# Mixture sums in PSUM, earlier weights for the last merge row, and a re-timed residual scaling in a hybrid encoder layer

## The chip, the core and the metric

One core of a Trainium2 chip runs the whole layer in one launch. The metric is the device time of a run in microseconds (us), lower is better. PE is TensorE, DVE VectorE, ACT ScalarE, POOL GpSimd, SP the engine that issues the DMAs.

## What is computed

1,024 positions of 1,024 channels pass through one layer: two parallel branches (latent attention A, and RWKV-7 time mixing B), a gated mixture, a merge, and a gated MLP with a three-tap convolution. All of it is fp32. The part that matters here:

```
gates = sigmoid(gate_cols + b_gate)
x = x + (gates[0] * y_a + gates[1] * y_b) @ w_merge
h = rms_norm(x, norm_ffn_g)
gp = dwconv_centered(h @ w_ffn_gate, ffn_conv_w, ffn_conv_b)
x = x + (silu(gp) * (h @ w_ffn_up)) @ w_ffn_down
```

with y_a = A @ w_o[:512] and y_b = B @ w_o[512:].

## The kernel before

Activations lie with channels on the 128 partitions, positions along the free dimension. A **row** below is one tile of 128 output channels by 1,024 positions; it fills two PSUM banks of 512 positions. fp32 precision comes from splitting: each operand x becomes hi = x rounded to fp32r (a copy on ACT) and lo = x - hi (a subtraction, `split`, line 211), and each product is three matmuls, hi*hi, hi*lo, lo*hi. A weight tile is loaded raw (`wraw`), ACT makes `whi`, POOL makes `wlo` (`wload`, line 217); raw, hi and lo have two buffers each.

After both branches, gates[0]*y_a lies in DRAM as eight rows `d_y0`, and the gate logits as `d_gate`. The stages that the change touches:

- **Mixture**, `mixture(j)`, line 1641, rows j = 0 to 7. It loads y0 and the gate logits gt (two buffers each, used in turn), and multiplies four k-tiles of B by w_o (`product`, line 1377). In `branch` (line 1394) ACT takes the sigmoid of gt in place, and DVE multiplies the two PSUM banks into gt. Then DVE adds y0, ACT copies the sum to `yh`, and DVE subtracts for `yl`. Until `yl` is done, gt is not free for the load of row j+2.
- **Merge**, the loop at line 1711: row j is eight k-tiles of yh, yl times w_merge, 48 matmuls of 512 columns, in two weight halves of four k-tiles. `residual` (line 1707) adds x (loaded into `x2` at line 1658); ACT and DVE then make scaled and split forms for the FFN (`scaled`, `sums`) and squares for the norm (`squares`). Row 7 is written apart (line 1772), behind row 6's followers.
- **FFN**, 22 hidden tiles f. Each gate and up tile is computed by a scheme of seven quarter products on sums and differences of weight and activation blocks (U1 to U4, B11 to B22), made by DVE and POOL. `ones` times `acc` sums the squares; ACT forms irs = sqrt(mean + eps) and rs2 = 1/irs by Ln and Exp. `over` (1826) multiplies the rows of x2 by irs on POOL, since the result is multiplied by rs2 at the very end; `into` (1869) adds the down product of a row to x2, so row j must be scaled ahead of it (rows 0 to 3 in f = 2, rows 4 to 7 in f = 3). `taps` (two DVE operations over 1,023 columns), `silu`, `left` and `right` form the hidden tile.

PSUM has two sets of four banks, and `big4` (1636) takes a pair from one set and the other in turn. The second set opens at line 1653, behind row 1, so row 3 gets row 0's banks, and a later row j those of row j-4.

The order of PE is the order of the code. Up to the end of merge row 6 a scheduler orders the other engines by readiness and free buffers; from line 1733 on all engines follow the code. Each engine, and SP's queue of DMA issues, runs in order.

Of the kernel before, what the change touches and what calls it, by code (L numbers as in the profile page):

```python
# [13 lines left out]
AF = mybir.ActivationFunctionType  # L14
# [5 lines left out]
D = 1024  # L20
# [66 lines left out]
def block_kernel(ctx: ExitStack, tc: tile.TileContext, a):  # L87
# [64 lines left out]
    def act(out, in_, func, **kw):  # L152
        name = SETS.get(func)
        if name is None:
            return S.activation(out, in_, func, **kw)
        if name != cur["set"]:
            ld = S.preload_act_table_set(name)
            if "ordered" in cur:
                cur.update(set=name)
                return S.activation(out, in_, func, **kw)  # L160
            for g in cur["group"]:
                tc.add_manual_dep(ld.ins, g.ins.name, NOSYNC, reason="table set order")
            if cur["load"] is not None and not cur["group"]:
                tc.add_manual_dep(ld.ins, cur["load"].ins.name, NOSYNC, reason="table set order")
            cur.update(set=name, load=ld, group=[])
        i = S.activation(out, in_, func, **kw)
        if "ordered" in cur:
            return i
        tc.add_manual_dep(i.ins, cur["load"].ins.name, NOSYNC, reason="table set order")
        cur["group"].append(i)  # L170
        return i
# [39 lines left out]
    def split(x, hi, lo, eng=None):  # L211
        S.copy(hi, x)
        (eng or G).tensor_tensor(out=lo, in0=x, in1=hi.bitcast(F32), op=sub)
# [508 lines left out]
    def parts(idle=False):  # L722

        while True:
            e = None
            for i, (live, run, todo, pace) in enumerate(lanes):
                while len(run) < live and todo:
                    run.append([now[0], todo.pop(0), i])
                for x in run:
                    if e is None and (idle or now[0] >= last[i] + pace) and (x[0] in rkv if isinstance(x[0], tuple) else x[0] <= now[0]):  # L730
                        e = x
            if e is None:
                if not idle or not any(run for _, run, _, _ in lanes):
                    return
                now[0] = min(e[0] for _, run, _, _ in lanes for e in run)
                continue
            i = e[2]
            last[i] = now[0]
            x = next(e[1], None)
            if x is None:  # L740
                lanes[i][1].remove(e)
            else:
                e[0] = x if isinstance(x, tuple) else now[0] + DELAY[x]
# [625 lines left out]
    first = []  # L1369

    def wrows(src, k, n):
        return wload(src[:, k * 128:min(k + 4, n) * 128], 128 * min(4, n - k), bufs=2)
# [21 lines left out]
    def branch(br, j, xs, ps, gt):  # L1394

        if br:
            gate_load(br, j, gt)
        for k, ns in enumerate(product(ps, w_o(br, j), xs, NPAIR, br == 0)):
            if k == (1 + br):
                act(gt, gt, AF.Sigmoid, bias=vc("bgate", 8 * br + j))  # L1400
            elif k == 3:
                for x, hs in zip(ps, HT):
                    V.tensor_tensor(out=gt[:, hs], in0=x, in1=gt[:, hs], op=mult)
            yield ns

    fetched = []
# [229 lines left out]
    def big4():  # L1636
        nps[0] += 1
        return [psc[nps[0] % len(psc)].tile([128, 512], F32, tag="b4", name="b4") for _ in HT]

    sP.close()  # L1640
    def mixture(j):

        y0 = bq.tile([128, T], F32, tag=f"b{j % 2}", name="y0")
        nc.sync.dma_start(y0, d_y0[j])
        y = bq.tile([128, T], F32, tag=f"b{2 + j % 2}", name="gt")
        yield from branch(1, j, xs, big4(), y)
        V.tensor_tensor(out=y, in0=y, in1=y0, op=add)
        split(y, *yx[j], V)

    two_ = [mixture(j) for j in range(2)]  # L1650
    for i in (0, 0, 0, 1, 1, 1, 0, 0, 1, 1):
# [55 lines left out]
    def residual(j, ps):  # L1707
        for p, hs in zip(ps, HT):
            V.tensor_tensor(out=p, in0=p, in1=x2[j][:, hs], op=add)

    for j in range(7):
        ps = big4()
        for _ in product(ps, a["w_merge"][j], yx):
            pass
        residual(j, ps)
        k, g = j % 4, vc("gffn", j)
        y1, y2_ = ps
        scaled((B11 if j < 4 else B21)[k], y1, g)
        if j < 4:
            d = t5("p1")  # L1720
            S.copy(d, y1)
            V.tensor_tensor(out=d, in0=y2_, in1=d, op=sub)
            scaled(U1[k], d, g)
        else:
            t3, t2 = sums(j, ps, scaled_b12(j))
            split(t3, *U3[k], V)
            split(t2, *U2[k], V)
            scaled(B22[k], y2_, g)
        squares(j, ps)
# [95 lines left out]

    def over(js):
        for j in js:
            G.tensor_tensor(out=x2[j][:, :], in0=x2[j][:, :], in1=irs, op=mult)

    def load_next(f):  # L1830
        x11 = load("w_fu", f, 0, f5("AA"))
# [91 lines left out]
    e0()  # L1923
    e1 = u4(1)
    w7a = parts(s3)
    e1()
    bb1 = db[0]
    quarter(bb, w6a, U2, True)
# [2 lines left out]
    e2 = u4(2)  # L1931
    w7b = parts(b21)
    e2()
    for hs, b in zip(HT, db[1:]):
        act(irs[:, hs], b, AF.Ln, scale=1.0 / D, bias=eps)
    G.tensor_tensor(out=s2, in0=a12, in1=s2, op=sub)
    G.tensor_tensor(out=s1b, in0=b12, in1=s1b, op=sub)
    quarter(bb1, w6b, U2, True)
    spare = fp.tile([128, T], F32, tag="sh", name="u2b", bufs=3)
    u2b, u3b = (spare[:, hs] for hs in HT)  # L1940
# [3 lines left out]
    quarter(bb, w7a, U3)  # L1944
    e3()
    w4a = parts(a22)
    act(rs2, irs, AF.Exp, scale=-0.5)
    act(irs, irs, AF.Exp, scale=0.5)
    quarter(bb1, w7b, U3)
    u3a = t5("u3")  # L1950
    V.tensor_tensor(out=u3a, in0=bb, in1=p1a, op=add)
# [33 lines left out]
    right(0, ba[0], bc[0], u2a, lambda: W.append(parts(x[1])))  # L1985
    u2 = t5("u2")
    V.tensor_tensor(out=u2, in0=bb, in1=p1, op=add)
    over((0, 1))
    taps(1, u, 0)
    taps(1, u, 1)  # L1990
    s22 = x[2]
# [2 lines left out]
    for f in range(2, NF):  # L1994
        b, c, last = ba[f % 2], bc[f % 2], f == NF - 1
        f0, j0 = (f // 2 - 1) * 2, f % 2 * 4
        d2 = load_down(f0, j0 + 2)
        if f > 2:
            quarter(b, W.pop(0), B11, True)
            right(f - 1, ba[1 - f % 2], bc[1 - f % 2], u2, lambda: W.append(parts(s3)))  # L2000
            quarter(bb, W.pop(0), U2, True)
            p1 = t5("p1")
            S.copy(p1, b)
            W.append(parts(d1, G))
            u2 = t5("u2")
            V.tensor_tensor(out=u2, in0=bb, in1=p1, op=add)
        else:
            W.append(parts(d1, G))
            silu(1)
            left(1, ba[1])  # L2010
            right(1, ba[1], bc[1], u2b)
        quarter(b, W.pop(0), B21)
        G.tensor_tensor(out=s2, in0=x12, in1=s2, op=sub)
        W.append(parts(s1))
        if f < 4:
            over(((2, 3), (6, 7))[f - 2])
        if last:
            d1 = load_down(NF - 2, 0)
        quarter(bb, W.pop(0), U3)
        W.append(parts(s22))  # L2020
        u3 = t5("u3")
        V.tensor_tensor(out=u3, in0=bb, in1=p1, op=add)
        W.append(parts(d2, G))
        if last:
            d2 = load_down(NF - 2, 2)
        else:
            x = load_next(f + 1)
        for v in units(W.pop(0), j0):
            e = dbank()
            for k in range(2):  # L2030
                down(v, f0, k, e)
            into(v, e)
        quarter(c, W.pop(0), U1, True)
        W.append(parts(s2))
        if not last:
            s1 = sums_next(*x)
        V.tensor_tensor(out=u3, in0=c, in1=u3, op=add)
        u = u22(u3)
        quarter(bb, W.pop(0), U4)
        W.append(parts(d1, G) if last else parts(x[0]))  # L2040
        if last:
            d1 = load_down(NF - 2, 4)
        else:
            s2 = diffs_next(x[0], x[1], s1)
        if f == 2:
            over((4, 5))
        u21(u, bb, p1)
        if not last:
            W.append(parts(s2))
        center(f, u)  # L2050
        todo = []
        for v in units(W.pop(0), j0 + 2):
            e = dbank()
            for k in range(2):
                down(v, f0, k, e)
            todo.append((v, e))
            if len(todo) < 3:
                into(*todo[-1])
                taps(f, u, len(todo) - 1)
            else:  # L2060
                into(*todo[-1])
        if last:
            W.append(parts(d2, G))
            d2 = load_down(NF - 2, 6)
        else:
            x12 = load("w_fu", f + 1, 1, f5("AA"))
            d1 = load_down(((f + 1) // 2 - 1) * 2, (f + 1) % 2 * 4)
        quarter(c, W.pop(0), B22)
        W.append(parts(d1, G) if last else parts(x12))
        silu(f)  # L2070
        left(f, b)
        s3, s22 = x[1], x[2]
# [115 lines left out]
```

## Time and profile before

| what | us |
|---|---|
| median of 3 runs (lowest, highest) | 1938.6 (1937.78, 1941.22) |
| the profiled execution, its own time | 1937.92 |
| its span, first to last instruction | 1936.1 |
| PE busy (share of the span) | 1841.8 (95%) |
| DVE, ACT, POOL busy | 1229.6, 871.1, 655.4 |
| mean granted TensorE clock | 0.974 of full |

The profile lists for each engine its instructions in order of time, with the idle time ahead of one and the engine whose work ended it. A lost microsecond counts only where PE, or what PE waits for, is on the chain that ended last. The mixture runs from about 1103 to 1149 us of the span, the merge from there to 1251, the first FFN steps to 1334.

### The profile page before, as it was taken

The page shows a single profiled execution, that of the slowest core. Times are in us where ns is not written, and L with a number is a line of the kernel's source. Part 1 is how long each engine was busy: PE and PEld are TensorE (multiplying, and loading weights), DVE is VectorE, ACT ScalarE, POOL GpSimd, SP SyncE. Part 2 cuts the span into 40 slices and gives each one's busy share as a digit, 9 for nine tenths or more (in the row PEclk, how much of TensorE's full clock was granted, in tenths as well). Part 3 has the DMA queues.
Part 4 walks back from the last instruction along what each step waited for, and adds up shares of the span by engine and source line. Part 5 has one row for each costly group of instructions (what it writes and reads, how often), then busy time and mean ns, then how long its engine had stood idle before and what let it go on. Part 6 is the DMA issues. An engine that isn't in the chain of part 4 may idle for free. (4 is left out here: it accounts for less than half of the span.)

```text
span 1936.1 us, 36734 instructions
## 1 busy us (share of the span) xinstructions
PE 1841.8 (95%) x14928; PEld 1467.8 (76%) x14928; DVE 1229.6 (64%) x1837; ACT 871.1 (45%) x1380; POOL 655.4 (34%) x558
## 2 busy tenths in 40 slices
PE   6889999999999999989999999988999999999998
PEld 5657666888788877767777777767888888888886
DVE  7567665445556686766573264687766757667567
ACT  5676567223233565655666444442323333233231
POOL 7435554421222333352533322236222222222321
PEclk9989999999999999997999999999999999999999
DMA  4135544954555645453435672101111111111112
GB/s 158 37 120 193 181 157 147 252 140 99 142 144 122 148 110 137 101 139 84 104 83 174 213 250 87 55 33 55 50 56 59 49 50 52 63 50 50 49 55 103
DMA packets 260632, 210.65 MB, mean 109 GB/s; under 512 B 127144, under 2 KB 205032, under 8 KB 260464
## 3 DMA queue, kind: packets, MB, share of 16 engines
q1 hardware_dynamic: 260464, 208.31, 36.4%
q8 instruction: 117, 1.92, 0.4%
q14 instruction: 51, 0.42, 0.1%
HBM read 144.64 MB, written 59.41 MB: 105 GB/s over the span
## 5 line engine op out<-in xcount | busy, mean ns | idle before, releaser
L108 POOL TENSOR_TENSOR wlo<-wraw,whi 128x512 fp32r<-128x512 f32 x118 | 162.2, 1375 | 586.9 <-ACT whi L108 580.1
L123 PE MATMUL st<-hh,whi 128*128 128x512 f32 x408 | 172.4, 422 | 15.1 <-ACT hh L108 9.5
L123 PE MATMUL st<-hl,whi 128*128 128x512 f32 x408 | 163.6, 401 | 0.7 <-DVE hl L108 0.7
L108 DVE TENSOR_TENSOR x<-b,x 128x512 f32<-128x512 f32 x176 | 119.0, 686 | 54.9 <-PE b L123 54.9
L123 PE MATMUL st<-hh,wlo 128*128 128x512 f32 x408 | 140.3, 398 | 0.7 <-POOL wlo L108 0.7
L108 POOL TENSOR_TENSOR pl<-pe,ph 128x512 fp32r<-128x512 f32 x64 | 83.1, 1300 | 165.3 <-ACT ph L108 154.6
L108 ACT CAST whi<-wraw 128x512 fp32r<-128x512 f32 x118 | 72.9, 618 | 110.3 <-issue 30.4
L123 PEld LDWEIGHTS st<-hh,whi 128*128 128x128 f32 x408 | 78.9, 193 | 43.6 <-issue 10.9
L108 DVE TENSOR_REDUCE mx<-sc 128x1 f32<-128x512 f32 x128 | 81.8, 682 | 28.3 <-PE sc L123 28.1
L123 PEld LDWEIGHTS st<-hh,wlo 128*128 128x128 f32 x408 | 78.4, 192 | 19.1 <-POOL wlo L108 1.5
L123 PEld LDWEIGHTS st<-hl,whi 128*128 128x128 f32 x408 | 79.1, 194 | 17.7 <-DVE hl L108 1.6
L108 POOL TENSOR_TENSOR wl<-wraw,wh 128x512 fp32r<-128x512 f32 x22 | 28.9, 1313 | 179.7 <-ACT wh L108 174.8
L108 DVE TENSOR_TENSOR u<-b,p 128x512 f32<-128x512 f32 x42 | 29.0, 690 | 71.7 <-PE b L123 71.7
L123 PE MATMUL b<-sh,wh 128*128 128x512 f32 x176 | 69.3, 394 | 2.6 <-ACT sh L108 2.6
L123 PE MATMUL b<-sl,wh 128*128 128x512 f32 x176 | 69.1, 393 | 0.8 <-DVE sl L108 0.8
L123 PE MATMUL b<-sh,whi 128*128 128x512 f32 x176 | 68.6, 390 | 1.3 <-DVE x L108 1.3
L123 PE MATMUL b<-sh,wl 128*128 128x512 f32 x176 | 69.2, 393 | 0.0
L123 PE MATMUL b<-sh,wlo 128*128 128x512 f32 x176 | 68.5, 389 | 0.0
L123 PE MATMUL b<-sl,whi 128*128 128x512 f32 x176 | 68.5, 389 | 0.0
L108 DVE TENSOR_TENSOR pl<-st,ph 128x512 fp32r<-128x512 f32 x64 | 43.6, 683 | 28.3 <-ACT st L108 27.9
L108 ACT CAST whi<-s 128x512 fp32r<-128x512 f32 x33 | 20.5, 622 | 89.1 <-PE b L123 89.1
L123 PE MATMUL po<-ph,vhh 128*128 128x512 f32 x128 | 58.3, 455 | 1.8 <-ACT rc L108 1.8
(487 smaller groups left out, 5360.9 us busy)
## 6 DMA issues: line engine op xcount, KB each, us to landing
wraw<-w_in SPq DMA_DIRECT2D x64, 256.0 KB
wraw<-w_fd SPq DMA_DIRECT2D x44, 256.0 KB
AA<-w_fu SPq DMA_DIRECT2D x41, 256.0 KB
A<-w_fg SPq DMA_DIRECT2D x41, 256.0 KB
ld<-d_x SPq DMA_DIRECT2D x32, 256.0 KB
d_gate<-gt SPq DMA_DIRECT2D x32, 256.0 KB
xt<-xT SPq DMA_DIRECT2D x8, 512.0 KB
d_s<-sg SPq DMA_DIRECT2D x8, 512.0 KB
```

The source lines that it names most:

```text
L108: return f(*args, **kw)
L123: return f(out, a, b, **kw)
```

## The change

- In the mixture, the gate product and the sum with y0 stay in the PSUM banks; the split reads them there, bank by bank. gt is free after the two products, y0 after the two sums, the banks only after the split.
- The weights of merge row 7 are split ahead of row 6's residual in the code.
- `over` works in pieces of 512 columns. Rows 0 and 1 are scaled ten quarter products earlier, rows 2 and 3 later, together with 4 and 5.
- Ln of the mean square goes into PSUM in place, earlier; irs (Exp, 0.5) follows before the quarter of w6b, and rs2 (Exp, -0.5) is taken from PSUM in two halves, each apart.

```diff
--- before.py
+++ after.py
@@ -1400,7 +1400,7 @@
                 act(gt, gt, AF.Sigmoid, bias=vc("bgate", 8 * br + j))
             elif k == 3:
                 for x, hs in zip(ps, HT):
-                    V.tensor_tensor(out=gt[:, hs], in0=x, in1=gt[:, hs], op=mult)
+                    V.tensor_tensor(out=x if br else gt[:, hs], in0=x, in1=gt[:, hs], op=mult)
             yield ns
 
     fetched = []
@@ -1643,9 +1643,11 @@
         y0 = bq.tile([128, T], F32, tag=f"b{j % 2}", name="y0")
         nc.sync.dma_start(y0, d_y0[j])
         y = bq.tile([128, T], F32, tag=f"b{2 + j % 2}", name="gt")
-        yield from branch(1, j, xs, big4(), y)
-        V.tensor_tensor(out=y, in0=y, in1=y0, op=add)
-        split(y, *yx[j], V)
+        ps = big4()
+        yield from branch(1, j, xs, ps, y)
+        for x, hs in zip(ps, HT):
+            V.tensor_tensor(out=x, in0=x, in1=y0[:, hs], op=add)
+            split(x, *(t[:, hs] for t in yx[j]), V)
 
     two_ = [mixture(j) for j in range(2)]
     for i in (0, 0, 0, 1, 1, 1, 0, 0, 1, 1):
@@ -1712,6 +1714,8 @@
         ps = big4()
         for _ in product(ps, a["w_merge"][j], yx):
             pass
+        if j == 6:
+            first.extend([wrows(a["w_merge"][7], k, 8) for k in (0, 4)])
         residual(j, ps)
         k, g = j % 4, vc("gffn", j)
         y1, y2_ = ps
@@ -1825,7 +1829,8 @@
 
     def over(js):
         for j in js:
-            G.tensor_tensor(out=x2[j][:, :], in0=x2[j][:, :], in1=irs, op=mult)
+            for hs in HT:
+                G.tensor_tensor(out=x2[j][:, hs], in0=x2[j][:, hs], in1=irs[:, hs], op=mult)
 
     def load_next(f):
         x11 = load("w_fu", f, 0, f5("AA"))
@@ -1923,6 +1928,8 @@
     e0()
     e1 = u4(1)
     w7a = parts(s3)
+    for hs, b in zip(HT, db[1:]):
+        act(b, b, AF.Ln, scale=1.0 / D, bias=eps)
     e1()
     bb1 = db[0]
     quarter(bb, w6a, U2, True)
@@ -1931,10 +1938,11 @@
     e2 = u4(2)
     w7b = parts(b21)
     e2()
-    for hs, b in zip(HT, db[1:]):
-        act(irs[:, hs], b, AF.Ln, scale=1.0 / D, bias=eps)
     G.tensor_tensor(out=s2, in0=a12, in1=s2, op=sub)
     G.tensor_tensor(out=s1b, in0=b12, in1=s1b, op=sub)
+    for hs, b in zip(HT, db[1:]):
+        act(irs[:, hs], b, AF.Exp, scale=0.5)
+    over((0, 1))
     quarter(bb1, w6b, U2, True)
     spare = fp.tile([128, T], F32, tag="sh", name="u2b", bufs=3)
     u2b, u3b = (spare[:, hs] for hs in HT)
@@ -1944,8 +1952,8 @@
     quarter(bb, w7a, U3)
     e3()
     w4a = parts(a22)
-    act(rs2, irs, AF.Exp, scale=-0.5)
-    act(irs, irs, AF.Exp, scale=0.5)
+    for hs, b in zip(HT, db[1:]):
+        act(rs2[:, hs], b, AF.Exp, scale=-0.5)
     quarter(bb1, w7b, U3)
     u3a = t5("u3")
     V.tensor_tensor(out=u3a, in0=bb, in1=p1a, op=add)
@@ -1985,7 +1993,6 @@
     right(0, ba[0], bc[0], u2a, lambda: W.append(parts(x[1])))
     u2 = t5("u2")
     V.tensor_tensor(out=u2, in0=bb, in1=p1, op=add)
-    over((0, 1))
     taps(1, u, 0)
     taps(1, u, 1)
     s22 = x[2]
@@ -2012,8 +2019,8 @@
         quarter(b, W.pop(0), B21)
         G.tensor_tensor(out=s2, in0=x12, in1=s2, op=sub)
         W.append(parts(s1))
-        if f < 4:
-            over(((2, 3), (6, 7))[f - 2])
+        if f == 3:
+            over((6, 7))
         if last:
             d1 = load_down(NF - 2, 0)
         quarter(bb, W.pop(0), U3)
@@ -2043,7 +2050,7 @@
         else:
             s2 = diffs_next(x[0], x[1], s1)
         if f == 2:
-            over((4, 5))
+            over((2, 3, 4, 5))
         u21(u, bb, p1)
         if not last:
             W.append(parts(s2))
```

Three places show how the instructions move. **SP, the DMA issues around the last gates of the mixture** (y is y0, x the residual rows, w_merge the merge weights in halves). Before:

```order
L1644 DMA y_13347<-d_y_119 128x1024
L220 DMA wraw<-w_merge 128x512
L1390 DMA gt<-d_gate_81 128x1024
L1658 DMA x_13017<-xT 128x1024
L1658 DMA x_13018<-xT 128x1024
L1658 DMA x_13019<-xT 128x1024
L1658 DMA x_13020<-xT 128x1024
L1658 DMA x_13021<-xT 128x1024
L1658 DMA x_13022<-xT 128x1024
L1658 DMA x_13023<-xT 128x1024
L1658 DMA x_13024<-xT 128x1024
L220 DMA wraw<-w_merge 128x512 x13
```

and now:

```order
L1644 DMA y_13323<-d_y_118 128x1024
L1390 DMA gt<-d_gate_81 128x1024
L1660 DMA x_13017<-xT 128x1024
L1660 DMA x_13018<-xT 128x1024
L1644 DMA y_13368<-d_y_119 128x1024
L1660 DMA x_13019<-xT 128x1024
L1660 DMA x_13020<-xT 128x1024
L1660 DMA x_13021<-xT 128x1024
L1660 DMA x_13022<-xT 128x1024
L1660 DMA x_13023<-xT 128x1024
L1660 DMA x_13024<-xT 128x1024
L220 DMA wraw<-w_merge 128x512 x15
```

The second half of merge row 0 now stands behind all eight loads of x; before, both halves of row 0 and one of row 1 stood ahead of them. The y0 of row 7 stands behind two of them.

**ACT, merge rows 6 and 7** (b21h, t3h, b22h, p belong to row 6's followers; the two casts of whi are row 7's weights). Before:

```order
L108 ACTIVATE b_13813<-b_13813 128x512
L108 ACTIVATE b21h<-b_13896,vec 128x512
L108 CAST t3h_13418<-u_13964 128x512
L108 ACTIVATE b22h<-b_13897,vec 128x512
L108 ACTIVATE p_13984<-x_13020,vec 128x512
L108 CAST whi<-wraw 128x512 x2
L108 COPY x_13023<-b_13896 128x512
L108 ACTIVATE b_13896<-b_13896 128x512
L108 CAST t2h_13414<-u_13965 128x512
L108 COPY x_13023<-b_13897 128x512
```

and now:

```order
L108 ACTIVATE b_13837<-b_13837 128x512
L108 CAST whi<-wraw 128x512 x2
L108 ACTIVATE b21h<-b_13920,vec 128x512
L108 CAST t3h_13442<-u_14000 128x512
L108 ACTIVATE b22h<-b_13921,vec 128x512
L108 ACTIVATE p_14020<-x_13020,vec 128x512
L108 COPY x_13023<-b_13920 128x512
L108 ACTIVATE b_13920<-b_13920 128x512
L108 CAST t2h_13438<-u_14001 128x512
L108 COPY x_13023<-b_13921 128x512
```

Both casts now stand ahead of row 6's first follower.

**POOL, first FFN steps** (x times irs is `over`; s, s1b, A are weight sums and differences, wl and wlo low halves of weights). Before:

```order
L108 TENSOR_TENSOR s_14373<-s_14366,AA 128x512
L108 TENSOR_TENSOR A_14308<-AA,A_14308 128x512
L108 TENSOR_TENSOR x_13017<-x_13017,irs 128x1024
L108 TENSOR_TENSOR x_13018<-x_13018,irs 128x1024
L108 TENSOR_TENSOR wl<-wraw,wh 128x512
L108 TENSOR_TENSOR s_14373<-ra,s_14373 128x512
L108 TENSOR_TENSOR x_13019<-x_13019,irs 128x1024
L108 TENSOR_TENSOR x_13020<-x_13020,irs 128x1024
L108 TENSOR_TENSOR wlo<-wraw,whi 128x512
```

and now:

```order
L108 TENSOR_TENSOR s1b<-AA,s1b 128x512
L108 TENSOR_TENSOR x_13017<-x_13017,irs 128x512 x2
L108 TENSOR_TENSOR x_13018<-x_13018,irs 128x512 x2
L108 TENSOR_TENSOR s_14396<-A_14338,A_14340 128x512
L108 TENSOR_TENSOR s_14403<-s_14396,AA 128x512
L108 TENSOR_TENSOR A_14338<-AA,A_14338 128x512
L108 TENSOR_TENSOR wl<-wraw,wh 128x512
L108 TENSOR_TENSOR s_14403<-ra,s_14403 128x512
L108 TENSOR_TENSOR wlo<-wraw,whi 128x512
```

and some rows further:

```order
L108 TENSOR_TENSOR s_14596<-A_14548,A_14550 128x512
L108 TENSOR_TENSOR s_14617<-s_14596,AA 128x512
L108 TENSOR_TENSOR A_14548<-AA,A_14548 128x512
L108 TENSOR_TENSOR x_13019<-x_13019,irs 128x512 x2
L108 TENSOR_TENSOR x_13020<-x_13020,irs 128x512 x2
L108 TENSOR_TENSOR x_13021<-x_13021,irs 128x512 x2
L108 TENSOR_TENSOR x_13022<-x_13022,irs 128x512 x2
L108 TENSOR_TENSOR wl<-wraw,wh 128x512
```

Rows 0 and 1 (x_13017, x_13018) move ahead of the weight sums of f = 2; rows 2 and 3 now stand behind those of f = 3, with rows 4 and 5.

## Rows read from the trace of the kernel before

**Rows 1.** The chain of work that ended last, in order of time: start, length (us), engine, what.

```profile
1152.40 4.02 DMA gt<-d_gate
...
1164.72 67.86 PE b L123 x292
...
1334.15 577.63 PE b L123 x2547
```

**Rows 2.** PE in order of time over mixture and merge: start, length of the stretch (us), the matmul and how many, and in brackets the idle time ahead of it and what ended it.

```profile
1116.11 0.39 PE L123 MATMUL b<-obh,whi 128*128 128x512 f32 x1
...
1148.75 0.39 PE L123 MATMUL b<-yh,whi 128*128 128x512 f32 x1
...
1158.64 0.50 PE L123 MATMUL b<-yh,whi 128*128 128x512 f32 x1 [1.57 <-ACT yh L108]
1160.16 0.50 PE L123 MATMUL b<-yl,whi 128*128 128x512 f32 x1 [1.02 <-DVE yl L108]
...
1170.08 0.39 PE L123 MATMUL b<-yh,whi 128*128 128x512 f32 x1
...
1175.52 0.39 PE L123 MATMUL b<-yh,whi 128*128 128x512 f32 x1
...
1237.10 0.79 PE L123 MATMUL b<-yh,whi 128*128 128x512 f32 x1 [4.30 <-ACT whi L108]
...
1250.80 0.39 PE L123 MATMUL b<-b11h,whi 128*128 128x512 f32 x1
```

**Rows 3.** Stretches of time: length, then busy time and number of instructions of PE, PEld, DVE, ACT and POOL, the granted TensorE clock (1.00 is full), the DMA engines' busy share, GB/s.

```profile
1154.00:1166.00 12.00, 7.55 (x24) 4.78 (x23) 7.26 (x6) 3.65 (x4) 2.38 (x2) 0.79 1.00 404
1160.50:1167.50 7.00, 5.14 (x13) 3.19 (x12) 3.72 (x4) 1.04 (x1) 0.75 (x1) 0.53 0.94 371
1236.50:1242.50 6.00, 5.40 (x13) 4.24 (x14) 3.00 (x5) 3.54 (x8) 2.52 (x2) 0.50 0.41 131
1317.80:1321.20 3.40, 3.40 (x10) 2.68 (x9) 2.79 (x5) 0.64 (x2) 1.43 (x1) 0.52 0.21 77
```

**Rows 4.** DVE in order of time, in the mixture (columns as in rows 2).

```profile
1117.61 1.29 DVE L108 TENSOR_TENSOR gt<-b,gt 128x512 f32<-128x512 f32 x2 [13.05 <-ACT gt L108]
...
1122.41 2.31 DVE L108 TENSOR_TENSOR gt<-gt,y 128x1024 f32<-128x1024 f32 x1
```

**Rows 5.** ACT in order of time: a gate's sigmoid in the mixture, the end of merge row 6, the root.

```profile
1118.72 1.16 ACT L108 ACTIVATE gt<-gt,vec 128x1024 f32<-128x1024 f32 x1 [1.15 <-DMA gt<-d_gate]
...
1233.34 0.69 ACT L108 ACTIVATE b21h<-b,vec 128x512 fp32r<-128x512 f32 x1 [5.21 <-DVE b L108]
...
1236.44 1.12 ACT L108 CAST whi<-wraw 128x512 fp32r<-128x512 f32 x2
...
1273.93 1.27 ACT L108 ACTIVATE irs<-b,cst 128x512 f32<-128x512 f32 x2
```

**Rows 6.** All instructions on the low weight halves: durations are shortest/median/longest in ns, then first and last start.

```profile
L108 POOL TENSOR_TENSOR wlo<-wraw,whi x118: 1264/1289/2366, 50.9 to 1908.3; 128x512 fp32r<-128x512 f32 x118
```

**Rows 7.** DVE in order of time, in the first FFN steps.

```profile
1264.41 1.75 DVE L108 TENSOR_TENSOR t4l<-u,t4h 128x512 fp32r<-128x512 f32 x1
...
1275.73 0.69 DVE L108 TENSOR_TENSOR wlo<-AA,whi 128x512 fp32r<-128x512 f32 x1 [1.79 <-ACT whi L108]
...
1282.52 0.69 DVE L108 TENSOR_TENSOR wl<-A,wh 128x512 fp32r<-128x512 f32 x1 [2.12 <-ACT wh L108]
...
1294.58 2.87 DVE L108 TENSOR_TENSOR wl<-s,wh 128x512 fp32r<-128x512 f32 x1
1297.38 2.88 DVE L108 TENSOR_TENSOR u<-u2b,rs 128x512 f32<-128x512 f32 x1
...
1307.50 5.54 DVE L108 SCALAR_TENSOR_TENSOR cvb<-u,vec,cvb 128x1023 f32<-128x1023 f32 x2
...
1327.81 2.88 DVE L108 TENSOR_TENSOR wl<-AA,wh 128x512 fp32r<-128x512 f32 x1
1330.61 0.68 DVE L108 TENSOR_TENSOR b<-b,p 128x512 f32<-128x512 f32 x1
...
1335.82 1.27 DVE L108 SCALAR_TENSOR_TENSOR cv<-u,vec,cv 128x1023 f32<-128x1023 f32 x1
```

**Rows 8.** POOL in order of time, in the same stretch.

```profile
1265.58 1.74 POOL L108 TENSOR_TENSOR s1b<-AA,s1b 128x512 f32<-128x512 f32 x1
...
1293.54 6.17 POOL L108 TENSOR_TENSOR x<-x,irs 128x1024 f32<-128x1024 f32 x2
...
1308.61 6.65 POOL L108 TENSOR_TENSOR x<-x,irs 128x1024 f32<-128x1024 f32 x2
...
1327.29 5.66 POOL L108 TENSOR_TENSOR x<-x,irs 128x1024 f32<-128x1024 f32 x2
...
1345.03 5.66 POOL L108 TENSOR_TENSOR x<-x,irs 128x1024 f32<-128x1024 f32 x2
```

**Rows 9.** PE in order of time, in the same stretch.

```profile
1307.73 0.76 PE L123 MATMUL b<-t3h,whi 128*128 128x512 f32 x1 [2.89 <-DVE u L108]
...
1315.60 0.49 PE L123 MATMUL b<-sh,wh 128*128 128x512 f32 x1 [2.63 <-ACT sh L108]
...
1316.90 0.50 PE L123 MATMUL b<-sl,wh 128*128 128x512 f32 x1 [0.81 <-DVE sl L108]
...
1334.15 0.50 PE L123 MATMUL b<-sh,whi 128*128 128x512 f32 x1 [1.30 <-DVE x L108]
```

## The prediction, made before the changed kernel had run

> **What bounds the kernel now.** I read the chain that ended last first. From 1334 us to nearly the end it is one block of matmuls, 577.63 us long, which no part of the change touches; ahead of it the chain leaves PE often [rows 1]. So I read PE in order of time over the three touched stages, and looked for idle time and for matmuls that follow each other at a slower pace. Four k-tiles of a merge row (24 matmuls) take 1175.52 - 1170.08 = 5.44 us when nothing waits, a whole row 10.88, a mixture row 5.44 [rows 2].
>
> *Merge.* Its eight rows should take 87.0 us; from 1148.75 to 1250.80 they take 102.0 [rows 2]. Of the 15.0 lost, row 7 has 7.1: PE sits idle for 4.30 us until ACT has made its weights, and then needs 13.7 us rather than 10.88, since the granted clock is 0.50 for about 6 us [rows 2, 3]. The other 7.9 lie in row 0, which waits for yh and yl of the last mixture rows and then runs at clock 0.53 for 7 us [rows 2, 3]. The clock has two levels, 1.2 and 2.4 GHz, and both low stretches follow such waits. The chain names the cause in row 0: the last gate is issued at 1152.40, 3.6 us after PE has finished the mixture, as its buffer had been held until yl, and takes 4.02 us to land [rows 1, 2].
>
> *First FFN steps, 1250.8 to 1334.* Here PE waits for DVE, and DVE is slow where `over` runs on POOL. A DVE operation of 512 columns with both inputs in SBUF takes 2.87 and 2.88 us beside POOL's 1,024-column pieces, against 0.69 otherwise [rows 7, 8]. Beside a 512-column POOL operation it takes 1.75 [rows 7, 8]. With one input in PSUM it takes 0.68 even while `over` runs [rows 7, 8].
>
> **The change, part by part.**
>
> *1. Mixture sums in PSUM (removes row 0's waits).* gt is free after the two products, some 1.3 us behind the row's last matmul. Add a load of 4.0 and a sigmoid of 1.16 [rows 1, 5]: the gate of row j+2 is ready 6.5 us after row j, and is wanted after 10.9. PE no longer waits for gates, and the 7.9 us go. DVE now has six operations of 512 per row; at 0.65 each (1.29 for two [rows 4]) this is 3.9 us, under PE's 5.44. The old sum over 1,024 columns took up to 2.31 [rows 4].
>
> Two new waits take their place.
> - *Row 3 needs row 0's banks.* DVE starts row 0's products at 1117.61 [rows 4], and they and the sums last to 1120.1. Row 1's gate is ready at 1119.9 [rows 5], its products are done at 1121.4; behind them on DVE come yl of row 0 (first bank, 1122.0), a sum (1122.6), yl (second bank, 1123.2). PE wants row 3's second bank at 1116.11 + 5.44 + 0.45 = 1122.0 [rows 2]. Cost 1.3 us; bounds 0, if row 1's gate lands sooner, and 3, if ACT's copies come late.
> - *The second weight half of merge row 0* is now issued behind the last gate, eight loads of x and the y0 of row 7: 5.5 MB with itself. At 404 GB/s [rows 3] that is 13.6 us, and 1.5 more until the first of it flows (from the last gate's 4.02 for 0.5 MB [rows 1]). The last gate goes out when row 5's products are done: 1116.11 + 4 x 5.44 + 1.3 + 1.3 = 1140.5; so the half lands at 1155.6. ACT's cast (two take 1.12 [rows 5]) makes it 1156.2. Row 0's fifth k-tile is wanted at 1116.11 + 6 x 5.44 + 1.3 + 5.44 = 1155.5. PE waits 0.7, then 0.5 more for `wlo` (1.29 on POOL [rows 6]), with restarts 1.5. Bounds: 0 where the loads run a little faster, 3.5 where 2 us later, and 3.4 more if the clock falls for another 7 us.
>
> The row's 404 GB/s speaks for the shorter wait. The Trainium skill, "SBUF — State Buffer", "Summary: rules for kernel authors", reckons with about 358 GB/s between HBM and SBUF; by that the half lands 1.8 us later, PE waits 3.3, and the sum below comes to 1921.3. The trace disagrees with it over those 12 us.
>
> Part 1: 7.9 - 1.3 - 1.5 = 5.1 us gained.
>
> *2. Row 7's weights split ahead of row 6's followers.* ACT is idle for 5.21 us before 1233.34 [rows 5], so the first cast, whose buffer PE frees half way through row 6, costs nothing; the second waits for row 6's last matmul, as does the residual behind it on ACT, which wants DVE's addition first. So nothing is late next, and row 7 starts at once at full clock: 7.1 us (4.3 if the clock falls for another reason).
>
> *3. `over` in other places.* All times below are those of before, so earlier is relative to part 2.
> - *Rows 0 and 1, new place.* irs now follows at the place of the old Ln (1273.93 [rows 5], without the table load ahead of it, moved to where ACT idles), and four pieces run to about 1280. They block DVE operations at 1.75 - 0.69 = 1.06 each, 4.2 us at most. But DVE idled there for 1.79 and 2.12 us on ACT [rows 7], and ACT has 1.3 us less to do. I take 0.5 lost, between -1 and 4.2.
> - *Rows 0 and 1, old place.* Two blocked operations fall from 2.87 and 2.88 to 0.69 [rows 7]: 4.4 gained. PE's wait of 2.89 at 1307.73 [rows 9] starts 3.9 earlier.
> - *Rows 2 and 3, old place.* The pair of taps took 5.54 beside them, 2 x 1.27 free [rows 7]: 3.0. A POOL operation of 512 that stays there still blocks one of the two, for 1.1; 1.9 gained. PE's waits at 1315.60 and 1316.90 for sh and sl [rows 9] end 5.8 earlier.
> - *Rows 2 to 5, new place.* The operation at 1327.81 falls from 2.88 to 1.75 as the pieces are shorter; PE's 1.30 at 1334.15 shrinks by 1.1 [rows 7, 9]. The other four pieces run on to about 1342 and block DVE some 3 us more, which I take PE not to see: it runs without a wait from 1334 on, though `over` runs from 1345.03 beside it [rows 1, 8].
> - The Exp in halves: within ACT's idle time, nothing.
>
> Part 3: 3.9 + 1.9 + 1.1 = 6.9. The low clock from 1317.8 to 1321.2 [rows 3] I leave as it is; it is worth 1.7.
>
> Sum: 5.1 + 7.1 + 6.9 = 19.1 us off the profiled execution's 1937.9 (span 1936.1): 1918.8. The median of the runs is 0.7 above it, so **1919.5**.
>
> **Rivals.**
> - *Row 0 of the merge starves on.* The half lands over 2 us late, PE waits 3.5 and the clock falls for 7 us: part 1 gives -0.3, the sum 1925. For it: the loads stood in the queue to about 1167 before, and low clock followed a wait there [rows 2, 3]. Against: the loads now start 12 us earlier. The Trainium skill's page cited above lies on this side; without the clock's fall its rate gives 1921.3.
> - *Part 3 moves the blocking only.* Four pieces cost 4.2 in their new place and the later ones gain nothing: 2.1 rather than 6.9, 1924.3. For it: two DVE inputs in SBUF are blocked wherever `over` runs. Against: DVE's idle time there.
> - *Row 7's weights come no earlier*, as the cast waits for a buffer after all: 1926.6. Against: rows 1 to 6 have their casts in that place, and PE runs through their starts for 67.86 us [rows 1].
> - *Slower.* DVE becomes the bound of the mixture: if its PSUM operations are blocked as SBUF ones are (1.75), six take 10.5 us a row, 5.1 over PE's pace, 40 over eight rows: 1957. It decides from 1.45 us each on, where it eats the 21.9 of all parts and 3.9 more. Against: 0.68 beside `over` [rows 7].
>
> **How the numbers follow.** Forecast 0.63; starved row 0 0.15; part 3 without gain 0.12; row 7 without gain 0.04; two of these three together, near no change at the worst, 0.03; DVE-bound 0.03. A measurement of this kernel can tell 0.2%, 3.9 us, from no change. Faster 0.94, the same 0.03, slower 0.03. The range goes from 1911 (no new wait 2.8, no low clock 1.7, taps free 1.1, and PE's 2.89 at 1307.73 gone too) to 1929, which takes in each single rival but the last.
>
> **What would show it.** Right: matmuls of merge row 0 at an even pace except at its fifth k-tile; row 7 directly behind row 6; no DVE operation near 2.9 us in the first FFN steps; the solid block of PE starting about 19 us earlier, just as long. Wrong: waits of PE for yl or banks in each mixture row; a wait for `whi` over 3 us; low clock where it was full.

## The result, and the profile after

| | us |
|---|---|
| changed kernel, median of 4 runs (lowest, highest) | 1920.87 (1915.96, 1922.72) |
| kernel before, median of 4 runs | 1938.19 (1934.20, 1941.22) |
| ratio, 95% interval | 0.9906 (0.9883 to 0.9929) |
| profiled execution, its span | 1920.34, 1918.4 |
| forecast, its range | 1919.5, 1911 to 1929 |

One run of the kernel before, beside experiments 1 and 2, took 3572.2 us and is left out of every figure.

The time fell as forecast. The stages under it did not: the weight half of merge row 0 came late, as the first rival had it. In the profile below, code ahead of the change happened to run 3.5 us faster and hid part of that cost; in two later profiles the first FFN steps did, with 2.2 us more than forecast.

PE after, in order of time (columns as in [rows 2, 9]), with every wait from mixture row 2 on:

```profile
1118.45 0.50 PE L123 MATMUL b<-obh,whi 128*128 128x512 f32 x1 [0.21 <-DVE yl L108]
...
1119.65 0.50 PE L123 MATMUL b<-obh,whi 128*128 128x512 f32 x1 [0.46 <-DVE yl L108]
...
1155.73 0.80 PE L123 MATMUL b<-yh,whi 128*128 128x512 f32 x1 [3.59 <-ACT whi L108]
...
1218.31 0.39 PE L123 MATMUL b<-yh,whi 128*128 128x512 f32 x1
...
1229.19 0.39 PE L123 MATMUL b<-yh,whi 128*128 128x512 f32 x1
...
1240.07 0.39 PE L123 MATMUL b<-b11h,whi 128*128 128x512 f32 x1
...
1270.77 0.47 PE L123 MATMUL b<-t4h,wh 128*128 128x512 f32 x1 [1.57 <-ACT rs L108]
...
1292.00 0.47 PE L123 MATMUL b<-t3h,whi 128*128 128x512 f32 x1 [1.91 <-DVE u L108]
...
1297.89 0.80 PE L123 MATMUL b<-sh,wh 128*128 128x512 f32 x1 [2.22 <-ACT sh L108]
...
1299.19 0.79 PE L123 MATMUL b<-sl,wh 128*128 128x512 f32 x1 [0.51 <-DVE sl L108]
...
1316.40 0.50 PE L123 MATMUL b<-sh,whi 128*128 128x512 f32 x1 [0.33 <-DVE x L108]
```

Three things stand here. The four waits for yh and yl in merge row 0 are gone, and one of 3.59 us for `whi` is there in their place. Rows 6 and 7 of the merge (1218.31, 1229.19, then the FFN at 1240.07) take 10.88 us each, so row 7 waits for nothing. In the FFN steps PE's waits come to 1.57 + 1.91 + 2.22 + 0.51 + 0.33 = 6.5 us; before they were 12.3, the four of [rows 9] (7.6) and these:

```profile
1280.54 0.47 PE L123 MATMUL b<-t4h,wh 128*128 128x512 f32 x1 [0.61 <-DVE u L108]
...
1284.56 0.47 PE L123 MATMUL b<-t4h,wh 128*128 128x512 f32 x1 [1.00 <-DVE u2b L108]
...
1297.51 0.51 PE L123 MATMUL b<-t2h,wl 128*128 128x512 f32 x1 [1.34 <-DVE wl L108]
...
1302.24 0.50 PE L123 MATMUL b<-b21h,wlo 128*128 128x512 f32 x1 [1.68 <-DVE wlo L108]
```

The chain that ended last, after (as [rows 1]), leads from the loads of x through the late weight half to ACT's cast and the matmuls behind it:

```profile
1138.87 5.29 DMA x<-xT
1144.22 10.73 DMA wraw<-w_merge
1155.73 84.29 PE b L123 x359
...
1316.40 577.64 PE b L123 x2547
```

The solid block is as long as before, 577.64 us, and 17.75 us earlier. But 3.47 of these lie ahead of the change: mixture row 2 starts at 1112.64 rather than 1116.11, in code that is the same. Ahead of it the clock was low for 68 us rather than 75 (added up from windows). Half of such time is lost, so the 7 us would make 3.4 of the 3.5. That is an estimate and no full account: profiles with the same 68 us start row 2 up to 2.9 us apart. I therefore compare the **stretch** from the first matmul of mixture row 2 to the first of the solid block. The first changed instruction, a product on DVE, starts 1.5 us into it. Only the last scaled pieces lie behind it, and from the block's start the span goes on for 601.9 to 602.0 us in every kernel here but one (whole rows, 603.4).

Windows over the two low clocks that are left, and over the loads (columns as in [rows 3]):

```profile
1138.00:1140.00 2.00, 2.00 (x11) 1.65 (x10) 1.94 (x4) 1.70 (x4) 1.30 (x1) 1.00 0.43 98
...
1140.00:1154.00 14.00, 12.14 (x54) 9.73 (x52) 8.06 (x13) 3.81 (x6) 1.30 (x1) 1.00 1.00 398
1155.70:1162.70 7.00, 6.97 (x19) 5.58 (x20) 0.00 (x0) 0.62 (x1) 2.51 (x2) 0.60 0.24 75
1298.50:1305.50 7.00, 6.49 (x18) 4.99 (x18) 4.70 (x9) 2.14 (x4) 2.72 (x2) 0.56 0.11 37
```

Each belongs to a wait of PE, of 3.59 and 2.22 us. The first begins in the wait, some 1.3 us before PE goes on; that part of it costs nothing.

### The profile page after: what moved, and what is told of

It is laid out like the page before. It is cut to its first block, busy times and chain, and to the rows that moved or that the text cites. A ratio compares the mean times of both kernels' runs of the same rounds, so it can differ in the third digit from the quotient of the medians.

```text
span 1918.4 us, 36770 instructions
## 1 busy us (share of the span) xinstructions
PE 1832.6 (96%) x14928; PEld 1464.1 (76%) x14928; DVE 1220.6 (64%) x1853; ACT 871.5 (45%) x1390; POOL 654.1 (34%) x566
## 5 line engine op out<-in xcount | busy, mean ns | idle before, releaser
L123 PEld LDWEIGHTS st<-hl,whi 128*128 128x128 f32 x408 | 78.8, 193 | 17.6 <-DVE hl L108 1.7
```

The lines of the kernel that those rows point to most:

```text
L123: return f(out, a, b, **kw)
```

## The experiments

Each kernel's stretch, cut at the start of merge row 6 and at the first FFN matmul, all from one profiled execution each. The last column is the time in the stretch at the clock's lower level (1.2 GHz): (1 - granted clock) x 2 x length, added over windows of 2 us, those in which PE waits included.

| kernel | row 2 to merge row 6 | rows 6, 7 | FFN to block | stretch | low clock |
|---|---|---|---|---|---|
| before | 105.65 | 29.04 | 83.35 | 218.04 | 20.4 |
| before, again | 106.12 | 29.04 | 83.36 | 218.52 | 20.4 |
| changed | 105.67 | 21.76 | 76.33 | 203.76 | 13.7 |
| changed, again | 104.15 | 21.76 | 74.13 | 200.04 | 6.8 |
| changed, third | 103.92 | 21.76 | 74.26 | 199.94 | 6.8 |
| sums only | 105.27 | 27.78 | 83.16 | 216.21 | 13.6 |
| row 7 only | 105.30 | 21.76 | 83.39 | 210.45 | 13.6 |
| scaling only | 106.45 | 27.86 | 74.14 | 208.45 | 13.6 |
| half first | 100.32 | 21.75 | 74.13 | 196.20 | 3.4 |
| half first, pairs | 99.35 | 21.76 | 74.15 | 195.26 | 3.4 |
| the same, again | 99.13 | 21.76 | 74.22 | 195.11 | 3.4 |
| whole rows | 104.39 | 21.77 | 79.30 | 205.46 | 13.6 |
| whole rows, again | 102.90 | 21.76 | 79.37 | 204.03 | 10.2 |
| rows 0, 1 late | 104.01 | 21.76 | 74.93 | 200.70 | 6.8 |

Times have a scatter of their own: mixture row 2 starts between 1110.7 and 1120.1 us in these 14 profiles, and runs of one kernel lie up to 18 us apart. So the table says where something was gained, and the medians say whether it counts.

**1. The three parts, one at a time** (the kernel before with some pieces of the diff alone).

Sums only, `mixture` and `branch`:

```diff
-                    V.tensor_tensor(out=gt[:, hs], in0=x, in1=gt[:, hs], op=mult)
+                    V.tensor_tensor(out=x if br else gt[:, hs], in0=x, in1=gt[:, hs], op=mult)
...
+            V.tensor_tensor(out=x, in0=x, in1=y0[:, hs], op=add)
+            split(x, *(t[:, hs] for t in yx[j]), V)
```

> The kernel before with the mixture part of the change alone. Measure in the profile: from the first matmul of mixture row 2 to the first matmul of the solid block of PE (218.04 us before, 203.76 after the whole change). Theory: the 7.9 us that merge row 0 lost are gone, but row 3's banks (1.5), the wait for the second weight half of merge row 0 (3.6) and the low clock behind it (3) eat them: 218 +- 1.5, the time within 2 us of before. Rival (the sums in PSUM are worth what was forecast, and the loss of the whole change lies in its other parts): 213, 5 us less than before.

Measured: 1936.76 us, ratio 0.9986 (0.9966 to 1.0007). PE in order of time:

```profile
1116.94 0.50 PE L123 MATMUL b<-obh,whi 128*128 128x512 f32 x1 [0.42 <-DVE yl L108]
...
1153.34 0.79 PE L123 MATMUL b<-yh,whi 128*128 128x512 f32 x1 [2.72 <-ACT whi L108]
...
1231.54 0.79 PE L123 MATMUL b<-yh,whi 128*128 128x512 f32 x1 [4.31 <-ACT whi L108]
```

The waits of [rows 2] for yh and yl are gone and a wait of 2.72 for the weight half is there, with 6.8 us of low clock from its end on. Up to merge row 6 the gain is 0.4 to 0.9 us, not 5.1. Row 7's wait stays. Of the 1.8 us by which the stretch is shorter, 1.3 lie in rows 6 and 7, where the clock was low for 3.4 us rather than 6.8.

Row 7 only:

```diff
+        if j == 6:
+            first.extend([wrows(a["w_merge"][7], k, 8) for k in (0, 4)])
```

> The kernel before with the earlier split of merge row 7's weights alone. Theory: row 7 follows row 6 without a wait at full clock, nothing else moves: 7.1 us less in the measured stretch (210.9), the time 7 less. Rival (the low clock behind row 7's wait would have come anyway, or the gain is given back in the FFN steps, which wait for DVE): 4.3 less or under 2 less.

Measured: 1934.87 us, ratio 0.9981 (0.9962 to 1.0000). Rows 6 and 7 take 21.76 us rather than 29.04, a gain of 7.28 in its own column and of nothing in the FFN steps. The time shows less of it than the stretch, 3.7 us with an interval from 0 to 7.4.

Scaling only (all pieces of the diff on `over`, Ln and Exp):

```diff
+            for hs in HT:
+                G.tensor_tensor(out=x2[j][:, hs], in0=x2[j][:, hs], in1=irs[:, hs], op=mult)
...
+    over((0, 1))
...
-            over((4, 5))
+            over((2, 3, 4, 5))
```

> The kernel before with the scaling of x2 in pieces, at other places, and the root apart, alone. Theory: 7 us less in the stretch (211), all of it behind 1284 us: DVE operations near 2.9 us fall to 0.7 at the old place of rows 0 and 1, and the pair of taps from 5.5 to about 3.5. Rival (the gain came from row 7 starting FFN earlier, not from the blocking): under 3 less.

Measured: 1928.95 us, ratio 0.9943 (0.9923 to 0.9963). FFN to block takes 9.2 us less, where 7 had been expected. Its waits are 1.56, 1.90, 0.63, 0.80 and 0.67, against 12.3 us in all before: 6.7 from waits. The clock is low for 3.4 us in these steps rather than 6.8, worth 1.7; the remaining 0.8 stands in neither.

By their ratios the three give 2.7 + 3.7 + 11.0 = 17.4 us, and together, by the first ratio, 18.2. Each interval reaches some 4 us to either side, and within that no part needs another. In the stretch they give 1.8 + 7.6 + 9.6 = 19.0, and together 14.3, 18.0 and 18.1.

**2. The late half put first.** Theory: merge row 0's second half is late because it stands behind the loads of x in SP's queue. The edit puts both halves ahead of them:

```diff
+    first.extend([wrows(a["w_merge"][0], k, 8) for k in (0, 4)])
     for j in range(8):
         i = nc.sync.dma_start(x2[j][:, :], a["xT"][j * 128:(j + 1) * 128, :])
```

> The changed kernel, with merge row 0's weights asked for ahead of the loads of x in the code, so that their second half stands ahead of all eight x in SP's queue. Theory: no wait of PE for that half, no low clock in row 0: 6.5 us less than the changed kernel (197 in the stretch). Rival (the mixture's in-order chain on ACT and DVE is late by itself, and PE would wait for yl of rows 5 to 7 in place of the weights): a wait for yl of 2 us or more in row 0, under 3 us less.

Measured: 1920.53 us, ratio 0.9903 (0.9881 to 0.9926). The wait for row 0's half is gone, and the low clock with it; a wait of 0.33 for `whi` stands at the start of merge row 1. Row 2 to merge row 6 takes 100.32, and no wait for yl came in its place. That shows the cause. The time was hardly below that of the changed kernel's first four runs, though, where 6.5 us less had been expected, which left open whether the stretch counts; the next runs set them side by side.

**3. The changed kernel again, and both new waits removed.**

> The changed kernel once more, to see which of its waits recur. Theory (the queue makes the second weight half of merge row 0 late): PE waits for it again at row 0's fifth k-tile, 3 to 4 us, with a granted clock of 0.5 for some us behind the wait; from the start of mixture row 2 to the start of the solid block 203 to 206 us, as 203.8 in its first profile. Rival (that half was late once, by chance): a wait under 1.5 us, no low clock there, 197 to 199 us. Time 1918 to 1923 by the first, 1914 to 1917 by the second.

Measured: 1917.39 us, ratio 0.9881 (0.9856 to 0.9906). The wait for the half recurs, 3.08 us, and 2.96 in the third profile below: it is the queue, not chance. What varies is the clock behind it, low for 6.8 us in the first profile and 3.4 in the two others; the stretch, 200.0, is below the 203 to 206 expected. The wait for sh, 2.22 us with 6.8 of low clock, is 0.60 in both. There the low clock, 3.4 us, stands one wait earlier, behind u:

```profile
1289.42 0.47 PE L123 MATMUL b<-t3h,whi 128*128 128x512 f32 x1 [1.91 <-DVE u L108]
...
1295.29 0.51 PE L123 MATMUL b<-sh,wh 128*128 128x512 f32 x1 [0.60 <-ACT sh L108]
```

```profile
1291.57:1293.57 2.00, 2.00 (x6) 1.55 (x5) 1.17 (x1) 0.74 (x1) 0.00 (x0) 0.50 0.62 216
```

From the one matmul to the other it is 5.87 us here and 5.89 in the first profile, where the clock stayed full between them. So low clock behind u cost nothing: PE came to sh 1.6 us later and waited 1.6 less. What cost time in the first profile is the low clock behind sh.

The version with the half first, and with mixture rows 2 and 3 both in the second set of banks:

```diff
-        return [psc[nps[0] % len(psc)].tile([128, 512], F32, tag="b4", name="b4") for _ in HT]
+        return [psc[(nps[0] - 1) // 2 % len(psc)].tile([128, 512], F32, tag="b4", name="b4") for _ in HT]
```

> The changed kernel with both weight halves of merge row 0 issued ahead of the eight loads of x, and with mixture rows 2 and 3 both in the second set of banks, so that row 3 waits for nothing of row 0. The first edit alone brought the stretch from mixture row 2 to the solid block from 203.8 to 196.2 us in its profile, but its time (1920.5) hardly below the changed kernel's. Theory (part 1 is worth what was forecast once both new waits are gone): the waits of 0.2 and 0.5 for yl in row 3 go, merge row 0 starts 32.6 us behind mixture row 2 rather than 33.9, the stretch is 195 us, the time 5 to 8 us under that of the changed kernel in this comparison, about 1913. Rival (what the stretch shows is the luck of one execution's clock): the same waits gone, but the time within 2 us of the changed kernel's.

Measured: 1914.92 us, ratio 0.9873 (0.9848 to 0.9897). SP's queue, PE, and the window behind the wait:

```profile
1136.14 0.32 SPq L1390 DMA_DIRECT2D gt<-d_gate  x1
1136.56 0.38 SPq L220 DMA_DIRECT2D wraw<-w_merge  x1
1136.99 0.42 SPq L1661 DMA_DIRECT2D x<-xT  x1
```

```profile
1155.36 0.50 PE L123 MATMUL b<-yh,whi 128*128 128x512 f32 x1 [0.67 <-ACT whi L108]
...
1156.73 0.73 PE L123 MATMUL b<-yh,wlo 128*128 128x512 f32 x2 [0.17 <-POOL wlo L108]
```

```profile
1155.00:1162.00 7.00, 6.47 (x27) 5.06 (x28) 3.00 (x5) 5.29 (x10) 2.65 (x3) 1.00 0.22 75
```

The half goes out 0.4 us behind the last gate. What is left is a wait of 0.67 at the start of merge row 1, and behind that one the clock stays full. Row 3 waits for no bank: merge row 0 starts 32.64 us behind mixture row 2, as before the change. The time is 2.5 us under that of the changed kernel beside it, where 5 to 8 had been expected.

Both kernels once more, for the size of the difference:

> The changed kernel a third time: two profiles gave 203.8 and 200.0 us for the stretch, 197.0 and 196.4 with half of the low-clock time taken off. Expected: again a wait of 3 to 4 us for the second weight half of merge row 0, the stretch 200 to 204 us, 196 to 197 at full clock, the time 1917 to 1922 us.

> The changed kernel with both weight halves of merge row 0 ahead of the loads of x and rows 2 and 3 in one set of banks, again, to set its time against that of the changed kernel more closely (1914.9 against 1917.4 with overlapping intervals). Theory (both new waits cost time, and their low clock with them): stretch about 195 us, 3 to 6 us under the changed kernel's time. Rival (it is the clock's luck): no difference over 1 us in the medians of both sets of runs together.

Measured: 1922.21 us, ratio 0.9917 (0.9892 to 0.9941) for the changed kernel; 1916.41, ratio 0.9885 (0.9861 to 0.9909) for the version, 5.8 us apart. In each of the two comparisons the intervals overlap. All runs together, the medians are 1919.76 (15 runs) and 1915.05 (12 runs), 4.7 us apart; the means are 4.1 us apart, with a standard error of 1.6. The stretch differs by 4.8 us between 195.2 and 200.0. So the version is the fastest kernel here, by some 4 us, and that is what the half and the banks cost together. How it divides is open: the half alone (experiment 2) has 3.8 of the 4.8 in its stretch, but its mean time lies only 0.2 above that of the changed kernel, with a standard error of 1.5.

**4. Pieces and places of the scaling.** Whole rows of 1,024 columns at the new places:

```diff
-            for hs in HT:
-                G.tensor_tensor(out=x2[j][:, hs], in0=x2[j][:, hs], in1=irs[:, hs], op=mult)
+            G.tensor_tensor(out=x2[j][:, :], in0=x2[j][:, :], in1=irs, op=mult)
```

> The changed kernel with the scaling of the residual rows back in pieces of 1,024 columns, all at the new places. Theory (what blocks a DVE operation with two SBUF inputs is the length of the POOL operation beside it): the DVE operation ahead of the solid block takes about 2.9 rather than 1.8 us, PE's wait there rises from 0.7 to about 1.8, and one or two operations beside rows 0 and 1 take up to 2.9; 1 to 2.5 us slower than the changed kernel. Rival (the places are all that matters, the pieces nothing): within 0.5 us in the stretch, and no DVE operation near 2.9 us.

Measured: 1928.03 us, ratio 0.9939 (0.9917 to 0.9961), 10.6 us over the changed kernel beside it. Missed by far, so it was run again:

> The changed kernel with the residual rows scaled in pieces of 1,024 columns, again, since it lost 10.6 us of time where its profile showed 2 us more in the stretch at full clock and 1.1 in a wait for the square p right behind the solid block's start. Theory (longer waits for rs and sh bring the clock down more often): the same waits of about 3.0 for rs, 2.2 for sh, 1.3 at the solid block and 1.1 behind it, the stretch 203 to 206 us, the time 1924 to 1930. Rival (the first set was unlucky): the time within 4 us of the changed kernel's.

Measured: 1926.80 us, ratio 0.9943 (0.9921 to 0.9965). That is 4.6 us over the changed kernel of the same set, just outside the rival's 4. All runs together 1927.6 against 1919.8: the pieces alone are worth some 8 us, with 10.6 and 4.6 in the two sets. DVE, then PE, in the second profile:

```profile
1261.70 2.49 DVE L108 TENSOR_TENSOR wlo<-AA,whi 128x512 fp32r<-128x512 f32 x1 [0.20 <-ACT whi L108]
1264.11 2.88 DVE L108 SCALAR_TENSOR_TENSOR u<-x,vec,t2h 128x512 f32<-128x512 f32 x1
...
1311.36 2.89 DVE L108 TENSOR_TENSOR wl<-AA,wh 128x512 fp32r<-128x512 f32 x1
```

```profile
1270.44 0.47 PE L123 MATMUL b<-t4h,wh 128*128 128x512 f32 x1 [2.96 <-ACT rs L108]
...
1298.04 0.62 PE L123 MATMUL b<-sh,wh 128*128 128x512 f32 x1 [2.25 <-ACT sh L108]
...
1317.72 0.50 PE L123 MATMUL b<-sh,whi 128*128 128x512 f32 x1 [1.31 <-DVE x L108]
...
1328.62 0.50 PE L123 MATMUL b<-b21h,whi 128*128 128x512 f32 x1 [1.09 <-ACT p L108]
```

The blocked operations grew as the theory said, but PE's waits with them came to more than I had allowed: 2.96 for 1.57, 1.31 for 0.65 to 0.79, and a new 1.09 behind the start of the block, with 3.4 and 6.8 us of low clock behind the first two of those shown. FFN to block takes 5.2 us more, and the part from the block to the end of the span another 1.4.

Rows 0 and 1 at their old place, in pieces:

```diff
-    over((0, 1))
     quarter(bb1, w6b, U2, True)
...
     V.tensor_tensor(out=u2, in0=bb, in1=p1, op=add)
+    over((0, 1))
```

> The changed kernel with rows 0 and 1 scaled at their old place, ten quarter products later, in pieces of 512 columns. Theory (that place stood on PE's path): wl and u there take about 1.75 us each rather than 0.60, PE's wait for u rises from 1.9 to 4 us or more, and the stretch to the solid block grows by 2 to 4 us. Rival (the pieces alone would have freed it): it grows by under 1 us.

Measured: 1921.07 us, ratio 0.9900 (0.9877 to 0.9924). The stretch grew by 0.7 us from the 200.0 of the changed kernel's later profiles, so the theory falls and its rival stands. The time is 3.7 us above the changed kernel of the same set and 1.3 above all its runs together; what of that is more than scatter stays open. DVE and PE:

```profile
1285.38 1.79 DVE L108 TENSOR_TENSOR wl<-s,wh 128x512 fp32r<-128x512 f32 x1
1287.09 1.78 DVE L108 TENSOR_TENSOR u<-u2b,rs 128x512 f32<-128x512 f32 x1
```

```profile
1291.87 0.50 PE L123 MATMUL b<-b21h,wlo 128*128 128x512 f32 x1 [1.22 <-DVE wlo L108]
...
1297.35 0.47 PE L123 MATMUL b<-t3h,whi 128*128 128x512 f32 x1 [2.92 <-DVE u L108]
```

The blocked operations take 1.79 and 1.78 us as expected. PE waits 1.22 + 2.92 = 4.14 us for them, but no longer the 1.57 for rs: against 1.57 + 1.91 = 3.48 that is 0.7 more. The new place of rows 0 and 1 moves a wait rather than removing it.

**5. The kernel before again.**

> The kernel before once more, for a second profile of its touched stages: from mixture row 2 to the solid block it took 218.0 us, of which about 19 at a granted clock of 0.5. Theory (the waits of that stretch recur, only how long the clock stays low behind them varies): the same waits in merge rows 0 and 7 and the first FFN steps, the stretch 215 to 220 us, and with half of its low-clock time taken off it 208 to 209. Rival (the first profile was an unlucky one): under 213 us, a wait of row 0 or 7 missing.

Measured: 1940.84 us, ratio 1.0014 (0.9997 to 1.0030). The same waits, among them 4.31 in row 7, and the stretch 218.52. So the stretch of before is no luck of one execution. With the low clock's half taken off the two stretches are 207.8 and 208.3; 208 to 209 was expected.

## Why the prediction was right, and where it was not

**Part 1, forecast 5.1, measured 0 to 1.7** (105.65 us to 105.67, 104.15 and 103.92). Its first step held: no wait for yh, yl or gates is left in merge row 0. So did the price of row 3's banks, 1.3: merge row 0 starts 33.90 us behind mixture row 2 rather than 32.64. **The term that failed is "the second weight half of merge row 0", 1.5 us.** It cost a wait of 3.59 (2.96 to 3.08 in the two later profiles) and 6.8 (3.4) us of low clock at its end. A wait for `whi` over 3 us was one of the signs that the prediction itself had named for being wrong. SP's issues show how it came, in order of time:

```profile
1138.02 0.32 SPq L1390 DMA_DIRECT2D gt<-d_gate  x1
1138.39 0.90 SPq L1660 DMA_DIRECT2D x<-xT  x2
1139.40 0.36 SPq L1644 DMA_DIRECT2D y<-d_y  x1
1139.81 3.40 SPq L1660 DMA_DIRECT2D x<-xT  x6
1144.22 1.61 SPq L220 DMA_DIRECT2D wraw<-w_merge  x2
```

Counted from mixture row 2, the last gate was forecast at 24.4 us and went out at 25.4. The half was forecast to land at 39.5 and landed at 42.3 (1144.22 + 10.73 - 1112.64). PE wanted it at 39.5; 39.4 was forecast. So 1.0 came from the gate and 1.8 from the loads. These ran at 98 GB/s for the first 2 us and at 398 for the next 14, and the half shared the end of them with the first half of row 1, issued in the same row, which I had not counted. With that half they are 5.77 MB, 14.5 us at 398 GB/s where I had 13.6; 2.4 us of the 16.9 between the gate's issue and the half's landing are left for the start and the end, where I had 1.5. My own row for these 1.5, 4.02 us for 0.5 MB, leaves 2.7 when the 1.3 at 404 GB/s are taken off: I had taken too little. Hence the wait lies at the upper bound that I gave for "2 us later", 3.5, and the clock did fall: in this part the rival to which I gave 0.15 is what happened, though its time, 1925, is not what came. The Trainium skill ("SBUF — State Buffer", "Summary: rules for kernel authors") has about 358 GB/s for such loads. The wait that I worked out from it, 3.3, is close to the one measured, but not for that reason: the trace disagrees with the rate, 398 GB/s over 14 us.

**Part 2, forecast 7.1, measured 7.28.** Row 7 starts without a wait at full clock, and the splits moved behind it made nothing late.

**Part 3, forecast 6.9, measured 7.0, 9.2 and 9.1** (FFN to block). From the waits it is 12.3 - 5.5 = 6.7 in the later profiles. The terms can be read from DVE after (columns as in [rows 7]):

```profile
1264.24 1.78 DVE L108 SCALAR_TENSOR_TENSOR u<-x,vec,t2h 128x512 f32<-128x512 f32 x1
1266.05 1.67 DVE L108 TENSOR_TENSOR u<-u,t2l 128x512 f32<-128x512 f32 x1
...
1283.25 0.68 DVE L108 TENSOR_TENSOR wl<-s,wh 128x512 fp32r<-128x512 f32 x1
1283.85 0.68 DVE L108 TENSOR_TENSOR u<-u2b,rs 128x512 f32<-128x512 f32 x1
...
1291.78 3.56 DVE L108 SCALAR_TENSOR_TENSOR cvb<-u,vec,cvb 128x1023 f32<-128x1023 f32 x2
...
1311.02 1.77 DVE L108 TENSOR_TENSOR wl<-AA,wh 128x512 fp32r<-128x512 f32 x1
```

The two at the old place fell from 2.87 and 2.88 to 0.68, the pair of taps from 5.54 to 3.56, the last from 2.88 to 1.77: three of three as worked out. At the new place, beside POOL's four pieces, two operations take 1.78 and 1.67. They cost PE 1.57 us for rs, where PE waited 0.61 and 1.00 for u and u2b before; so nothing was lost where I had 0.5. (The profile puts this wait down to rs, which ended at 1270.66; the sum that frees PE's bank ended at 1270.63. Both stand behind the two blocked operations.) The Trainium skill ("SBUF — State Buffer", "SBUF: two separate sides") says why a piece's length counts: where a VectorE operation reads two SBUF inputs and a GpSimd one reads SBUF, the later of the two waits for the whole instruction of the other. The trace agrees: beside pieces of 512 the same `wl` takes 1.77 us, beside pieces of 1,024 2.89, and DVE's sums with one input in PSUM 0.68 to 0.69 beside either. What I failed to see is how the gain divides: I spoke of places, with 1.1 us for pieces; the pieces are worth some 8 us of time, the early place of rows 0 and 1 0.7 of the stretch.

**The clock.** I had left the low clock of the FFN steps as it was. It went from 6.8 us there to 3.4 in two profiles of three, and in these two it was the part behind sh, the one that costs time, that was gone. In the whole stretch it fell from 20.4 us to 13.7, 6.8 and 6.8.

**The sum.** Forecast 19.1 off the profiled execution; measured 17.6, of which 3.5 lie ahead of the change and 14.3 in the stretch (0 + 7.3 + 7.0), while what lies behind the block's start and outside the span is 0.2 longer. In the two later profiles the stretch gave 18.0 and 18.1 (1.5 to 1.7 + 7.3 + 9.1 to 9.2) against 218.0. So the time was hit with part 1 wrong by 3.4 to 5.1 us, and with scatter or clock in its place: that it came within 1.4 us was luck. The chance of 0.94 for faster was right for reasons that the runs showed: parts 2 and 3 alone carry it, each in its own stage.

## What to carry to other kernels

A buffer freed earlier moves whatever stands behind it in the in-order queue: list what is now issued ahead of the next thing that PE needs, and put the small urgent load in front of the large ones (here 0.26 MB ahead of 4.2 MB, some 3 us of wait). Where POOL works on SBUF beside DVE operations with both inputs there, the length of POOL's single instruction sets how long a DVE operation can be held (1.77 us beside 512 columns, 2.89 beside 1,024): cutting it in two gave more than moving it. And where the time of a run scatters by more than the effect, compare a stretch of the trace that starts behind the scatter, cut by stage, in several profiles.

## What the runs showed that I had not expected

- The same wait is followed by low clock of different length: with the wait for the half 6.8 us (3.59), 3.4 (3.08) and 3.4 (2.96); with 2.72 in sums only 6.8, but with 2.98 in the second profile of whole rows none, and with 0.67 none either. With the wait for sh, 2.22 us came with 6.8. So the length of a wait alone does not say what the clock does behind it.
- With whole rows, PE's waits in the FFN steps grew by 2.5 us (8.0 for 5.5) and by 1.1 behind the block's start, and the time by 8. Low clock, 3.4 to 6.8 us more of it in the stretch than in the two later profiles of the changed kernel, makes some of the rest; what makes the remainder stays open, and the two sets, 10.6 and 4.6, differ by more than it.
- The start of mixture row 2, behind 1,100 us of code that is the same everywhere, lies anywhere from 1110.7 to 1120.1 us, and follows the low clock ahead of it, though not closely: 61 us of it at 1110.9, 75 at 1116.1, 85 at 1120.1, but 68 both at 1112.6 and at 1115.5.
